# When the second layer's modulation steps run inside the first channel MLP: pace 1.0 and 0.6 in place of 0.65 and 0.72, and a rule that holds some of them back

## The chip, the cores and the metric

The kernel runs on one core of one Trainium2 chip. The time is what one execution takes on the device, in microseconds. Three executions of the kernel before took 2763.98, 2764.24 and 2766.1 us; their median is 2764.24 us.

## The reference

The reference is one step of a two-layer network over 1152 tokens (128 context tokens, 1024 latent tokens) of width 1024, all in float32. Each layer has a token mixer and then a channel MLP with a hidden width of 4096. Every sub-layer is normed, modulated, and added back through a gate:

```python
def adaln(cvec, w, b):
    m = jax.nn.silu(cvec) @ w + b
    return [t[:, None, :] for t in jnp.split(m, N_MOD, axis=-1)]

def sqrelu_mlp(h, w1, w2):
    return jnp.square(jax.nn.relu(h @ w1)) @ w2

    for i in range(DEPTH):
        sh1c, sc1c, gt1c, sh2c, sc2c, gt2c = adaln(ctx_cond, ada_w[i], ada_b[i])
        sh1l, sc1l, gt1l, sh2l, sc2l, gt2l = adaln(c, ada_w[i], ada_b[i])
        ...
        ctx = ctx + gt1c * o_ctx
        lat = lat + gt1l * o_lat
        h_ctx = rmsnorm(ctx, norm_mlp_g[i]) * (1.0 + sc2c) + sh2c
        h_lat = rmsnorm(lat, norm_mlp_g[i]) * (1.0 + sc2l) + sh2l
        ctx = ctx + gt2c * sqrelu_mlp(h_ctx, mlp_w1[i], mlp_w2[i])
        lat = lat + gt2l * sqrelu_mlp(h_lat, mlp_w1[i], mlp_w2[i])
```

The modulation (`adaln`) of the second layer depends on the conditioning vectors alone. It is a product of two vectors with a 1024 x 6144 matrix, and it is needed only when the second layer begins.

## The kernel before, in words

Activations are held transposed: eight tiles of 128 features by 1152 tokens, and the tokens in three blocks of 384 (j = 0, 1, 2). A float32 product is made of three matmuls: each operand is split in a high and a low part (ACT copies the high part, DVE subtracts it from the source to get the low part), and high x high, high x low and low x high are summed in PSUM. The helper lines are L238 (high part on ACT), L241 (low part on DVE), and L344 to L346 (the three matmuls). So every weight tile costs ACT and DVE an instruction, and so does every activation tile that a matmul reads.

**The channel MLP has two halves** (`part` 0 and 1), each a loop over 8 blocks of the hidden width. The first half (`block0`) does token block 0 in the plain way: four upward groups of 24 matmuls, then eight downward groups of 12. The second half (`block1`) does token blocks 1 and 2 together, with a seven-product scheme for the upward matmuls in place of eight. Its products have names (A11, S1, A12, S2, S4, S3, A22), two sets of seven to a block. The weight operand of a product is made by DVE from sums of weight blocks: these are the items of kind `comb`. The sums stand at L292, L293 (with A11) and at L298, L299 (with A12). The downward weights are items of kind `unit`, which need no sum. A product's result in PSUM (`quad`, three PSUM tiles to a set, out of four that the downward groups share) is read by ACT (L1300, L1304) or added to an earlier one by DVE (L1310), then passes ACT twice (relu L1269, square L1270) and becomes a high part `hidh` (ACT) and a low part `hidl` (DVE), which the downward matmuls (`bps`) read. DVE also adds each downward result to the residual (L537).

**What sets the order.** The instructions of each engine stand in the order in which this code issues them, and each engine takes its own in that order. After each product, and after each downward group or half group, `tick` is called. It splits the next weight items (up to 6 ahead in the second half, 3 in the first), takes a step of `ada` when a counter `pace` says so, and takes a step of the norm that is pending. A block of the first half has 12 ticks, a block of the second half 34: numbers 1 to 13 and 16 belong to products (`kind` 0); 14 and 15 are the first half groups of the first two downward columns (`begin`, `kind` 1); 17 to 22 are the rest of those two columns, in half groups; 23 to 34 are the other downward groups. Products and downward groups are 12 matmuls long, half groups 6. Low parts are put in a list (`late`) and issued at the next `flush`, so the `hidl` of a product stands behind the steps of the ticks up to the next product's eviction.

**A step of `ada`** is one row block of the second layer's modulation matrix: two DVE instructions (L377, `junk`<-`adav`,`bc`), each a product of a 128 x 256 tile of weights with a broadcast conditioning row, summed along the row, one for each of the two conditioning vectors; each of them is followed by an instruction that reads the accumulator. Then SP is told to load the tile for the step after the next (L409): there are two buffers for these tiles, so that load must wait until this step has read its own. There are 192 such steps. Four times, at the start of each quarter of the columns, two steps load and prepare the broadcast row `bc` (L371 on ACT, L372 on DVE). One step is taken before the blocks, so 201 calls in all run the generator to its last product. What is left after the last block would be drained at once.

SP issues all loads of weights (L232, 512 KB each) and of modulation tiles (L409, 128 KB each) in the order of the code.

Of the kernel before, what the change touches and what calls it, by code (L numbers as in the profile page):

```python
# [38 lines left out]
def kernel(  # L39
# [77 lines left out]
    items = []  # L117
# [91 lines left out]
    wst = {"load": 0, "split": 0, "use": 0}  # L209
# [120 lines left out]
    def w_ahead(depth=None, most=2):  # L330
        d = depth if depth is not None else (3 if wextra else 1)
        n = 0
        while wst["split"] < wst["use"] + d and n < most and w_split():
            n += 1
# [192 lines left out]
    def step(g):  # L527
        next(g, None)
# [10 lines left out]
    def qstep(queue):  # L539
        while queue:  # L540
            try:
                next(queue[0])
                return True
            except StopIteration:
                queue.pop(0)
        return False

    def qdrain(queue):
        while qstep(queue):
            pass  # L550
# [19 lines left out]
        return queue  # L570

    HC = {}
    ADA_PACE = (0.65, 0.72)

    def norm_t(i, j, k, t):
        l, sub = divmod(i, 2)
# [102 lines left out]
    with tc.manual_schedule():  # L679
# [579 lines left out]
        def mlp(l, pend, make_norm, yp, ada, early):  # L1259
# [13 lines left out]
            quads = {}  # L1273

            def product(part, q, name, w, tick):
                st = quads.setdefault(q, {})
                b, bank = W_H[name]
# [30 lines left out]
                else:  # L1308
                    t = st[at]
                    nc.vector.tensor_tensor(out=t, in0=p, in1=t, op=ALU.add)  # L1310
                    flush()
                    squared(at[0], at[1] + 1, t, True)
                tick(0)

            def b_mm(ps, w, j, k0=0, k1=4):
                mm3(ps, lambda k: w[0][:, k, :], lambda k: w[1][:, k, :], lambda k: hid[k, j], 4, k0, k1)

            def down(units, js, tick):
                for n in units:
                    w = w_next()  # L1320
                    for j in js:
                        ps = zps("bps")
                        b_mm(ps, w, j)
                        resid(l, 5, n, j, ps)
                        flush()
                        tick(1)
                    w_done(w)
# [4 lines left out]
            def block0(tick):  # L1332
                for n in range(4):
                    w = w_next()
                    ps = zps("aps1")
                    mm_k(ps, w, hact(0))
                    w_done(w)
                    flush()
                    t = stile("qt")
                    nc.scalar.activation(t, ps, AF.Relu)  # L1340
                    squared(n, 0, t, False)
                    tick(0)
                for p in range(4):
                    w = w_next()
                    pss = [zps("bps") for _ in range(2)]
                    for k0, k1 in ((0, 3), (3, 4)) if p == 0 else ((0, 4),):
                        for n2 in range(2):
                            b_mm(pss[n2], half_w(w, n2), 0, k0, k1)
                            if k1 < 4:
                                continue  # L1350
                            resid(l, 5, 2 * p + n2, 0, pss[n2])
                            flush()
                            tick(1)
                        flush()
                    w_done(w)

            def block1(tick, tail):
                ws, pss = [], {}

                def begin(n, j):  # L1360
                    pss[n, j] = zps("bps")
                    b_mm(pss[n, j], ws[n], j, 0, 2)
                    tick(1)

                def end(n, j):
                    b_mm(pss[n, j], ws[n], j, 2, 4)
                    resid(l, 5, n, j, pss.pop((n, j)))
                    flush()
                    tick(1)

                for q, name in UP:
                    if q != "u":
                        product(1, q, name, w_next(), tick)
                    elif not tail:
                        ws.append(w_next())
                        begin(name, 2)
                if tail:
                    return
                flush()
                for n in range(2):  # L1380
                    end(n, 2)
                for n in range(2):
                    begin(n, 1)
                    end(n, 1)
                for w in ws:
                    w_done(w)
                down(range(2, 8), (2, 1), tick)

            pace = [0.0]
# [4 lines left out]
            for part in range(2):  # L1394
                for blk in range(8):
                    last = blk == 7
                    count = [0]

                    def tick(kind):
                        count[0] += 1  # L1400
                        env["defer"] = True
                        w_ahead(*((3, 1) if part == 0 else (6, 2)))
                        env["defer"] = False
                        pace[0] += 0 if (part, blk) in ((0, 7), (1, 0)) else ADA_PACE[part]
                        if pace[0] >= 1:
                            pace[0] -= 1
                            step(ada)
                        if part == 0 and last and count[0] == 4:
                            env["room"] += 16
                        if part == 0 or blk > 0:  # L1410
                            qstep(pend)

                    if part == 0:
                        block0(tick)
                    else:
                        block1(tick, last)
                    if part == 0 or not last:
                        hid.clear()
                    if part == 0 and last:
                        qdrain(pend)  # L1420
                        pend.extend(early())
# [304 lines left out]
```

## Time and profile before

| | before |
|---|---|
| median of 3 runs | 2764.24 us (2763.98 to 2766.1) |
| the profiled execution's own time | 2765.05 us |
| its span, first to last instruction | 2763.3 us |
| PE busy (matmuls) | 2707.8 us, 98% |
| DVE busy | 1838.4 us, 67% |
| ACT busy | 1204.7 us, 44% |
| DMA, mean | 89 GB/s |
| granted TensorE clock, mean | 0.994 |

The sections of the profile used here are the windows (busy time of each engine in a stretch), the waits (engine and line, what they waited for, us in total, times, longest), the chain of waits in order of time, and the timeline of one engine (start, duration, engine, line, operation, tiles; in square brackets the idle time before it and what ended it). In the first channel MLP, the first half runs from about 841 to 1112 us of the span and the second half from about 1113 to 1596 us. The second channel MLP, which has no `ada`, has its second half from about 2233 to 2717 us. A matmul of 384 columns starts some 0.175 us after the one before it when nothing is waited for; its recorded duration of 0.34 us overlaps the next one's.

### The profile page before, as it was taken

To read this page: it belongs to the slowest core of one execution; us is meant where nothing else is said; L and a number is where in the kernel's file an instruction comes from. 1 tells how busy PE (TensorE), PEld (TensorE's weight loads), DVE (VectorE), ACT (ScalarE), POOL (GpSimd) and SP (SyncE) were. 2 spreads that over 40 slices of the span, in tenths; PEclk is the share of its full clock that TensorE was granted. 3 is DMA by queue.
4 is the path that set the end of the run, shared out by engine and by line. 5 is a ranking of instruction groups with operands and counts; after the bars stand their busy time and mean duration, and the time that the engine had idled before them with its cause. 6 is when DMAs were issued, how large, how long until landed. Compare 5 with 4: busy or idle time off the path is not lost.

```text
span 2763.3 us, 48985 instructions
## 1 busy us (share of the span) xinstructions
PE 2707.8 (98%) x19863; PEld 2633.9 (95%) x19863; DVE 1838.4 (67%) x3997; ACT 1204.7 (44%) x2118; POOL 56.0 (2%) x79
## 2 busy tenths in 40 slices
PE   7999999999999999999999999999999999999998
PEld 5999999999899999999999998999999999999998
DVE  5676777777867966687888773443675566655555
ACT  5444343343535544444444463231464454444444
POOL 0000000000000000000000000000000000000000
PEclk9999999999999999999999999999999999999999
DMA  6122211221214454233333320111234432211212
GB/s 231 52 70 62 76 57 64 69 67 60 83 59 130 154 159 148 81 104 111 111 109 119 98 71 31 61 37 39 85 122 123 129 100 76 78 62 62 69 62 69
DMA packets 113698, 245.13 MB, mean 89 GB/s; under 512 B 12736, under 2 KB 68416, under 8 KB 113472
## 3 DMA queue, kind: packets, MB, share of 16 engines
q1 hardware_dynamic: 113472, 242.00, 27.4%
q8 instruction: 156, 2.56, 0.4%
q14 instruction: 70, 0.57, 0.1%
HBM read 236.19 MB, written 5.77 MB: 88 GB/s over the span
## 4 chain that ended last, share of the span: by engine, by line
PE 85%; DVE 7%; ACT 3%; DMA 3%; issue 1%; POOL 0%; SPq 0%; POOLq 0%; DVEq 0%; ACTq 0%
PE bps L345 9%; PE bps L346 9%; PE bps L344 9%; PE zps L344 5%; PE zps L345 5%; PE quad L1287 5%; PE zps L346 5%; PE quad L1289 5%; PE quad L1288 5%; PE aps L346 3%; PE aps L345 3%; PE aps L344 3%; PE lps L893 1%; PE ups L344 1%; PE ups L346 1%
## 5 line engine op out<-in xcount | busy, mean ns | idle before, releaser
L537 DVE SCALAR_TENSOR_TENSOR x<-bps,mod,x 128x384 f32<-128x384 f32 (+2 forms) x512 | 249.1, 512 | 152.1 <-PE bps L346 150.5
L241 DVE TENSOR_TENSOR wlo<-wraw,whi 128x1024 fp32r<-128x1024 f32 x206 | 251.4, 1220 | 104.1 <-ACT whi L238 103.9
L344 PE MATMUL zps<-hh,whi 128*128 128x384 f32 x912 | 317.3, 348 | 3.2 <-ACT hh L492 3.2
L1287 PE MATMUL quad<-hc,wunit 128*128 128x384 f32 x896 | 306.0, 341 | 9.2 <-ACT qt L1300 4.8
L1289 PE MATMUL quad<-hc,wunit 128*128 128x384 f32 x896 | 304.6, 340 | 3.4 <-DVE wunit L241 3.4
L345 PE MATMUL zps<-hl,whi 128*128 128x384 f32 x912 | 306.6, 336 | 0.8 <-DVE hl L500 0.8
L346 PE MATMUL zps<-hh,wlo 128*128 128x384 f32 x912 | 306.2, 336 | 1.2 <-DVE wlo L241 1.2
L345 PE MATMUL bps<-hidl,wunit 128*128 128x384 f32 x896 | 301.1, 336 | 3.7 <-DVE hidl L241 3.7
L1288 PE MATMUL quad<-hc,wunit 128*128 128x384 f32 x896 | 303.5, 339 | 0.0
L344 PE MATMUL bps<-hidh,wunit 128*128 128x384 f32 x896 | 300.7, 336 | 0.0
L346 PE MATMUL bps<-hidh,wunit 128*128 128x384 f32 x896 | 300.6, 335 | 0.0
L238 ACT ACTIVATE wunit<-wraw 128x512 fp32r<-128x512 f32 x304 | 187.4, 624 | 246.5 <-PE bps L346 235.7
L238 ACT ACTIVATE whi<-wraw 128x1024 fp32r<-128x1024 f32 x206 | 216.9, 1053 | 131.4 <-DMA wraw<-w 84.5
L241 DVE TENSOR_TENSOR wunit<-wraw,wunit 128x512 fp32r<-128x512 f32 x304 | 205.9, 686 | 26.3 <-ACT wunit L238 26.3
L241 DVE TENSOR_TENSOR hidl<-qt,hidh 128x384 fp32r<-128x384 f32 x192 | 106.7, 556 | 171.8 <-ACT hidh L238 171.7
L345 PE MATMUL bps<-hidl,whi 128*128 128x384 f32 x640 | 215.4, 337 | 0.8 <-DVE hidl L241 0.6
L344 PE MATMUL bps<-hidh,whi 128*128 128x384 f32 x640 | 215.8, 337 | 0.0
L346 PE MATMUL bps<-hidh,wlo 128*128 128x384 f32 x640 | 215.1, 336 | 0.0
L344 PEld LDWEIGHTS zps<-hh,whi 128*128 128x128 f32 x912 | 171.7, 188 | 12.7 <-issue 4.9
L1287 PEld LDWEIGHTS quad<-hc,wunit 128*128 128x128 f32 x896 | 170.0, 190 | 13.7 <-ACT qt L1300 8.1
L345 PEld LDWEIGHTS zps<-hl,whi 128*128 128x128 f32 x912 | 171.8, 188 | 2.5 <-DVE hl L500 2.5
L1289 PEld LDWEIGHTS quad<-hc,wunit 128*128 128x128 f32 x896 | 170.0, 190 | 4.0 <-DVE wunit L241 4.0
(226 smaller groups left out, 5918.2 us busy)
## 6 DMA issues: line engine op xcount, KB each, us to landing
wraw<-w SPq DMA_DIRECT2D x256, 512.0 KB, 3.5
adav<-ada_w SPq DMA_DIRECT2D x320, 128.0 KB, 2.5
wraw<-w_in SPq DMA_DIRECT2D x40, 512.0 KB, 4.2
adar<-ada_w SPq DMA_DIRECT2D x16, 512.0 KB, 8.4
x<-xT SPq DMA_DIRECT2D x24, 192.0 KB, 4.8
x<-xT SPq DMA_DIRECT2D x8, 576.0 KB, 3.8
yT<-y SPq DMA_DIRECT2D x24, 192.0 KB, 1.9
wraw<-w_out SPq DMA_DIRECT2D x8, 512.0 KB, 3.9
```

What stands on the lines that cost most here:

```text
L238: nc.scalar.activation(w[0], src, AF.Copy)
L241: eng.tensor_tensor(out=w[1], in0=src, in1=w[0].bitcast(F32), op=ALU.subtract)
L344: nc.tensor.matmul(ps, wh(k), ah, start=(k == 0), stop=False)
L345: nc.tensor.matmul(ps, wh(k), al, start=False, stop=False)
L346: nc.tensor.matmul(ps, wl(k), ah, start=False, stop=(k == n - 1))
L537: nc.vector.scalar_tensor_tensor(out=xs, in0=ps[:, a:b], scalar=g, in1=xs, op0=ALU.mult, op1=ALU.add)
L893: nc.tensor.matmul(ps[m * b:m * b + m, i, :], lhs[:, t0:t0 + m], rhs(c, b), start=True, stop=True)
L1287: nc.tensor.matmul(p, w[0][:, k, :], bh, start=(first and k == 0), stop=False, **go)
L1288: nc.tensor.matmul(p, w[0][:, k, :], bl, start=False, stop=False, **go)
L1289: nc.tensor.matmul(p, w[1][:, k, :], bh, start=False, stop=(k == 3), **go)
```

## The change

Two numbers and one condition. In the first channel MLP the counter now grows by 1.0 instead of 0.65 with each tick of the first half, and by 0.6 instead of 0.72 with each tick of the second half (not in the last block of the first half nor in the first block of the second, as before). And in the second half a tick after a product takes no step when the weight item that was split last is a `comb`; the counter keeps what it has, so the steps are taken at later ticks, one to a tick.

```diff
-    ADA_PACE = (0.65, 0.72)
+    ADA_PACE = (1.0, 0.6)
...
                         pace[0] += 0 if (part, blk) in ((0, 7), (1, 0)) else ADA_PACE[part]
-                        if pace[0] >= 1:
+
+                        if pace[0] >= 1 and (part == 0 or kind or items[min(wst["split"], len(items)) - 1][0] != "comb"):
                             pace[0] -= 1
                             step(ada)
```

No instruction is added or taken away; `junk` steps, their loads, and the eight preparations of `bc` change their places. The places that matter are on DVE.

The head of block 3 of the second half, first the kernel before, from the last step of the block ahead of it to the first `hidl` (`wunit` is a low part of a weight operand, `wraw` and `s` are sums of weight blocks, `qt` a product's result):

```order
L377 SCALAR_TENSOR_TENSOR junk,part<-adav,bc 128x256 x2
L292 TENSOR_TENSOR s_14562<-wraw 128x512
L293 TENSOR_TENSOR wraw<-wraw 128x512
L377 SCALAR_TENSOR_TENSOR junk,part<-adav,bc 128x256 x2
L241 TENSOR_TENSOR wunit<-wraw,wunit 128x512 x3
L298 TENSOR_TENSOR wraw<-wraw 128x512
L299 TENSOR_TENSOR wraw<-wraw 128x512
L377 SCALAR_TENSOR_TENSOR junk,part<-adav,bc 128x256 x2
L1310 TENSOR_TENSOR qt<-quad,qt 128x384
L241 TENSOR_TENSOR hidl<-qt,hidh 128x384
```

and the changed kernel:

```order
L241 TENSOR_TENSOR wunit<-wraw,wunit 128x512
L292 TENSOR_TENSOR s_14688<-wraw 128x512
L293 TENSOR_TENSOR wraw<-wraw 128x512
L241 TENSOR_TENSOR wunit<-wraw,wunit 128x512 x3
L298 TENSOR_TENSOR wraw<-wraw 128x512
L299 TENSOR_TENSOR wraw<-wraw 128x512
L1310 TENSOR_TENSOR qt<-quad,qt 128x384
L241 TENSOR_TENSOR hidl<-qt,hidh 128x384
```

The steps among the sums are gone; L1310 stands directly behind L299.

The same block from its last added product (S3 of the second set, L1310) to the first residual add. The kernel before:

```order
L1310 TENSOR_TENSOR qt<-quad,qt 128x384
L241 TENSOR_TENSOR hidl<-qt,hidh 128x384
L241 TENSOR_TENSOR wunit<-wraw,wunit 128x512
L377 SCALAR_TENSOR_TENSOR junk,part<-adav,bc 128x256 x4
L241 TENSOR_TENSOR hidl<-qt,hidh 128x384
L241 TENSOR_TENSOR wunit<-wraw,wunit 128x512
L377 SCALAR_TENSOR_TENSOR junk,part<-adav,bc 128x256 x2
L241 TENSOR_TENSOR hidl<-qt,hidh 128x384
L241 TENSOR_TENSOR wunit<-wraw,wunit 128x512
L537 SCALAR_TENSOR_TENSOR x_8132<-bps,mod,x_8132 128x384
```

and the changed kernel:

```order
L1310 TENSOR_TENSOR qt<-quad,qt 128x384
L241 TENSOR_TENSOR hidl<-qt,hidh 128x384
L241 TENSOR_TENSOR wunit<-wraw,wunit 128x512
L377 SCALAR_TENSOR_TENSOR junk,part<-adav,bc 128x256 x6
L241 TENSOR_TENSOR hidl<-qt,hidh 128x384
L241 TENSOR_TENSOR wunit<-wraw,wunit 128x512
L377 SCALAR_TENSOR_TENSOR junk,part<-adav,bc 128x256 x2
L241 TENSOR_TENSOR hidl<-qt,hidh 128x384
L241 TENSOR_TENSOR wunit<-wraw,wunit 128x512
L537 SCALAR_TENSOR_TENSOR x_8132<-bps,mod,x_8132 128x384
```

Three steps now stand ahead of the second `hidl` (that of S3) where there were two.

In the first half, a stretch of downward groups in block 2 (`hc` and `nt` belong to the pending norm). The kernel before:

```order
L537 SCALAR_TENSOR_TENSOR x_8132<-bps,mod,x_8132 128x256
L241 TENSOR_TENSOR hc<-nt,hc 128x384
L609 TENSOR_TENSOR ht<-nt,ht 128x384
L537 SCALAR_TENSOR_TENSOR x_8133<-bps,mod,x_8133 128x128
L537 SCALAR_TENSOR_TENSOR x_8133<-bps,mod,x_8133 128x256
L241 TENSOR_TENSOR wlo<-wraw,whi 128x1024
L377 SCALAR_TENSOR_TENSOR junk,mod<-adav,bc 128x256 x2
```

and the changed kernel:

```order
L537 SCALAR_TENSOR_TENSOR x_8132<-bps,mod,x_8132 128x256
L377 SCALAR_TENSOR_TENSOR junk,mod<-adav,bc 128x256 x2
L241 TENSOR_TENSOR hc<-nt,hc 128x384
L609 TENSOR_TENSOR ht<-nt,ht 128x384
L537 SCALAR_TENSOR_TENSOR x_8133<-bps,mod,x_8133 128x128
L537 SCALAR_TENSOR_TENSOR x_8133<-bps,mod,x_8133 128x256
L241 TENSOR_TENSOR wlo<-wraw,whi 128x1024
L377 SCALAR_TENSOR_TENSOR junk,mod<-adav,bc 128x256 x2
```

Every group's residual add now has a step behind it.

## The prediction

> **What bounds the kernel now.** I read the windows first, one for each half of the first channel MLP without its ends, and one for the second half of the other MLP, which has no modulation steps (columns: PE, PEld, DVE, ACT, POOL busy, granted clock, DMA share, GB/s).
>
> ```profile
> 874.00:1076.00 202.00, 202.00 (x1156) 202.00 (x1156) 156.88 (x392) 102.06 (x155) 0.00 (x0) 1.00 0.50 156
> 1145.00:1575.00 430.00, 421.73 (x2412) 417.96 (x2411) 343.77 (x981) 182.03 (x349) 0.00 (x0) 1.00 0.35 110
> 2260.00:2700.00 440.00, 438.39 (x2519) 436.32 (x2518) 258.25 (x433) 191.09 (x369) 0.00 (x0) 1.00 0.22 70
> ```
>
> PE sets the time in all three. Only the second has an idle PE that the steps could have caused: 8.3 us in 430, against 1.6 in 440 where there are none. The first half has no idle PE at all. So the most that moving steps can gain is about 8 us, 0.3% of the kernel. The waits of PE in that second window are two (us in total, times, longest):
>
> ```profile
> PE quad L1287 <- ACT qt L1300: 4.6, 5, 1.8
> PE bps L345 <- DVE hidl L241: 3.7, 5, 1.2
> ```
>
> Call them the head wait (a product waits for PSUM to be read) and the hid wait (a downward group waits for `hidl`). A modelled end makes each 0.17 us shorter than what it costs, so the ten of them cost 5.4 and 4.5 us. The chain of waits shows the head wait of block 3 (start, us, what):
>
> ```profile
> 1316.64 0.87 DVE junk L377 x4
> 1317.50 1.75 DVE wunit L241 x3
> 1319.25 0.61 DVE wraw L298
> 1319.89 0.69 DVE wraw L299
> 1320.58 0.79 DVE junk L377 x4
> 1321.37 0.42 DVE qt L1310
> ...
> 1323.93 0.39 ACT qt L1300
> 1324.37 0.44 PE quad L1287
> ```
>
> DVE is late with L1310 by its sums and by two steps (0.87 and 0.79 us with their accumulator reads); ACT, in order, reaches L1300 only behind what L1310 feeds. The hid wait of the same block, on DVE:
>
> ```profile
> 1341.49 0.56 DVE L1310 TENSOR_TENSOR qt<-quad,qt 128x384 f32<-128x384 f32 x1
> ...
> 1342.43 0.68 DVE L241 TENSOR_TENSOR wunit<-wraw,wunit 128x512 fp32r<-128x512 f32 x1
> 1343.44 0.43 DVE L377 SCALAR_TENSOR_TENSOR junk<-adav,bc 128x256 f32<-128x256 f32 x1 [0.32 <-DMA adav<-ada_w]
> ...
> 1345.37 0.43 DVE L377 SCALAR_TENSOR_TENSOR junk<-adav,bc 128x256 f32<-128x256 f32 x1 [1.06 <-DMA adav<-ada_w]
> ...
> 1346.10 0.55 DVE L241 TENSOR_TENSOR hidl<-qt,hidh 128x384 fp32r<-128x384 f32 x1
> ...
> 1347.76 0.43 DVE L377 SCALAR_TENSOR_TENSOR junk<-adav,bc 128x256 f32<-128x256 f32 x1 [0.51 <-DMA adav<-ada_w]
> ...
> 1348.50 0.55 DVE L241 TENSOR_TENSOR hidl<-qt,hidh 128x384 fp32r<-128x384 f32 x1
> ```
>
> Here it is not the steps' own 0.8 us that hold `hidl` up, but their loads: DVE stands in order behind a tile that is not there. With two buffers the load for a step can go out only when the step two before it is done.
>
> **The change part by part.** It moves 30 steps. In the first half 84 ticks count, so 54 steps become 84; 201 are needed in all, one comes ahead, so 146 in the second half become 116. No instruction goes away.
>
> *Head of the blocks, a gain.* Ticks 1 to 7 of blocks 1 to 6 take no step now, so both steps of that chain go. Block 3 has the longest wait (1.8 and 0.17 us), and without 0.87 + 0.79 it would lose 0.35; the other four share 3.4 us, and 0.8 or more less would leave them little. I take 0.4 left of 5.4: **-5.0 us**. It cannot gain more than 5.4.
>
> *Behind product S3, a loss.* The pause leaves 3 to 5 steps in the counter; they come out one to a tick, in ticks 8, 9 and 11 to about 20. That puts steps 13, 14 and 15 ahead of S3's `hidl` (the x6 row of the order), where one or two stood. The third needs a load that goes out when the first is done. In block 3 the trace shows when such a third step runs: the first (begun at 1343.44) was done 0.8 us later at 1344.3, its buffer's next step began at 1347.76 after a wait for the load, and DVE was free again at 1348.50. With the change `hidl` takes that place. PE's rows of the wait before:
>
> ```profile
> 1346.02 0.34 PE L344 MATMUL bps<-hidh,wunit 128*128 128x384 f32 x1
> 1346.71 0.44 PE L345 MATMUL bps<-hidl,wunit 128*128 128x384 f32 x1 [0.35 <-DVE hidl L241]
> ...
> 1539.57 0.34 PE L344 MATMUL bps<-hidh,wunit 128*128 128x384 f32 x1
> 1540.55 0.45 PE L345 MATMUL bps<-hidl,wunit 128*128 128x384 f32 x1 [0.64 <-DVE hidl L241]
> ```
>
> PE wanted it at 1346.20 (1346.02 and 0.175) and got it 0.61 us after `hidl` began (1346.10 to 1346.71). So it would get it at 1348.50 + 0.61 = 1349.11 and lose 2.9 us where it lost 0.5. In block 6 the first step's buffer was asked for anew and filled at
>
> ```profile
> 1537.48 5.38 SPq L409 DMA_DIRECT2D adav<-ada_w  x3
> 1541.62 0.43 DVE L377 SCALAR_TENSOR_TENSOR junk<-adav,bc 128x256 f32<-128x256 f32 x1 [0.52 <-DMA adav<-ada_w]
> ```
>
> that is 4.1 us on, behind a weight load of 512 KB that goes out just before it; with 0.74 for the step and 0.61 PE starts at 1542.97 in place of 1539.75 and loses 3.2. Block 4 has the preparation of a new `bc` row in ticks 14 and 15 in place of two steps, and waits for the row's load instead, which I count alike. Six blocks at 3.05 us are 18.3, less the 4.5 of before: **+13.8 us**. The bounds are those of the load:
>
> ```profile
> DMA to landing us min/median/max: 1.9/2.5/5.8
> ```
>
> With 2.5 in place of 3.5 to 4.1 a block loses about 1.5 (9 in all, +4.5); with 5.8 about 4.8 (29, +24). I take the rows of that very place.
>
> *The clock.* A PE that idles 2.7 us at a stretch six times is new in this MLP. Rows of elsewhere show what follows such a gap (PE's starts with the idle time ahead of them, and windows, where the granted clock stands third from the end):
>
> ```profile
> 47.68 1.13 PE L470 MATMUL rp<-rq,sel_sb 128*128 128x96 f32 x8 [2.13 <-DVE rq L463]
> ...
> 48.00:50.00 2.00, 2.00 (x16) 2.00 (x15) 0.62 (x2) 0.51 (x2) 0.00 (x0) 1.00 0.00 0
> ...
> 56.45 0.69 PE L344 MATMUL zps<-hh,whi 128*128 128x384 f32 x1 [2.06 <-ACT hh L492]
> ...
> 56.00:58.00 2.00, 1.51 (x4) 1.11 (x5) 1.84 (x4) 1.39 (x3) 0.47 (x2) 0.58 0.00 0
> 58.00:60.00 2.00, 2.00 (x8) 2.00 (x7) 2.00 (x4) 1.23 (x2) 0.81 (x1) 0.57 0.00 0
> ...
> 1116.57 0.41 PE L1287 MATMUL quad<-hc,wunit 128*128 128x384 f32 x1 [1.65 <-DVE x L537]
> ...
> 1118.84 0.69 PE L1289 MATMUL quad<-hc,wunit 128*128 128x384 f32 x1 [1.68 <-DVE wunit L241]
> ...
> 1122.20 0.52 PE L1287 MATMUL quad<-hc,wunit 128*128 128x384 f32 x1
> 1122.53 0.52 PE L1288 MATMUL quad<-hc,wunit 128*128 128x384 f32 x1
> ...
> 1124.00:1126.00 2.00, 2.00 (x12) 2.00 (x11) 1.44 (x3) 0.39 (x1) 0.00 (x0) 0.83 0.60 156
> ```
>
> A gap of 2.13 us left the clock at 1.00. One of 2.06 halved it: 0.58 and 0.57 as the means of two windows of 2 us are 3.4 us at 0.50. Two gaps close together, 3.3 us idle in all, halved it till about 1124.7 (0.83 is 0.7 us at 0.50), some 6 us from PE's start at 1118.84. At half clock matmuls start 0.32 us apart (1122.20 to 1122.53) in place of 0.175, so 3.4 us at half clock cost 1.5 and 6 us cost 2.7. Gaps of 2.7 lie between; I take three in four to halve it, 1.75 us each: 4.5 x 1.75 = **+7.9 us** (bounds 0 and 6 x 2.7 = 16). [...]
>
> *The first half.* 30 steps more at 0.85 us are 25 us of DVE in its seven counted blocks, 3.6 us in each block of 33.6. PE hides them where DVE has room. Block 2 is the tightest:
>
> ```profile
> 907.20:940.80 33.60, 33.60 (x194) 33.60 (x193) 31.38 (x79) 18.80 (x31) 0.00 (x0) 1.00 0.51 157
> ```
>
> 31.4 + 3.6 = 35.0 is 1.4 over, and what is over makes a `hidl` or a residual add late. Four PSUM tiles of 2.1 us each give some slack, and later blocks have room. I take **+1.5 us** (0 to 5).
>
> *Behind the hid wait.* Steps of ticks 16 to 21 come every 1.05 us, and the loads give one in about 2.4 (two buffers, 4 + 0.85 us a round). So residual adds (L537) fall some 6 us behind, which three more PSUM tiles just cover: **+0.8 us** (0 to 6). SP stands at these loads too, in order, with weight loads behind it:
>
> ```profile
> SPq L409 <- DVE junk L377: 244.7, 135, 22.0
> ```
>
> It did so before, and no engine waits for a weight load in this half (they are split six items ahead), so I put nothing on it.
>
> Sum, from the profiled execution's own 2765.05 us: -5.0 + 13.8 + 7.9 + 1.5 + 0.8 = +19.0, so 2784. The median of the runs shown lies 0.8 under that execution, which gives **2783 us**, 0.7% slower.
>
> **The rivals.** *The stalls come, the clock stays.* For it: the gap of 2.13 us did not lower it. Against: the one of 2.06 did. Without the 7.9 the time is 2775. [...] *The load is quick, nothing changes:* at 2.5 us a block loses 1.5, a gap too short for the clock: -5.0 + 4.5 + 1.5 = +1, 2765. For it: 2.5 is the median of all these loads. Against: rows of this very place show 3.5 to 4.1, and the weight load ahead of them stays. *Faster:* the pause lets DVE run ahead, and both buffers are full when the burst begins. If the third step needed no wait, three steps of 0.8 us would end 1.55 + 2.5 us after L1310 began, and `hidl` 0.55 later, at 4.6; PE wants it 4.7 after (1341.49 to 1346.20). Then both waits go: -5.0 - 4.5 + 1.5 = -8, 2756. Against: two buffers hold two tiles, and S3's L1310 cannot come sooner than S3. It decides if the load takes under 1 us. *Worse:* the first half overflows by 5, the residual adds by 6, and every gap halves the clock for 6 us: 2783 + 3.5 + 5.2 + 8.3 = 2800. *The change does not do what it says* (steps are left over and drained at the end): excluded, since the order has the last step in block 6.
>
> **How the numbers follow.** The forecast 0.50, clock stays 0.17, no change 0.13, faster 0.08, worse 0.12. A difference of 0.2% (5.5 us) is about what a measurement of this kernel can tell from none. Slower by more than that: 0.50 + 0.17 + 0.12, and a little of the quick load, 0.80; within it 0.12; faster 0.08. The range 2769 to 2798 holds the forecast with its bounds, the clock that stays and half of the worse case.
>
> **What would show it.** Right: the head wait (`quad` for ACT L1300) nearly gone in blocks 1 to 6; the hid wait (`bps` L345 for `hidl`) at 6 times, near 2.7 us each; three steps in a row ahead of it, the third waiting for `adav`; the clock under 1.00 in windows behind most of them; the idle PE of 874 to 1076 still under 2 us. Wrong: a hid wait of 1 us or none would fell the main term, a clock of 1.00 throughout the second one, and new waits in the first half or on PSUM behind L537 would mean that those terms are too small.

## The result, and the profile after

| | before | after |
|---|---|---|
| median, runs on the same chip | 2764.85 us (6 runs) | 2784.33 us (6 runs, 2783.6 to 2786.99) |
| ratio | | 1.0073, 95% interval 1.0063 to 1.0083 |
| profiled execution's own time | 2765.05 us | 2784.22 us |
| its span | 2763.3 us | 2782.4 us |
| PE busy | 2707.8 us | 2717.9 us |
| granted TensorE clock, mean | 0.994 | 0.99 |

The changed kernel is 0.7% slower: 2784.33 us where 2783 was predicted.

The three windows of the kernel after stand first: the first half of the first channel MLP, its second half, and the second half of the other MLP (columns: PE, PEld, DVE, ACT, POOL busy with the number of instructions, granted clock, DMA share, GB/s).

```profile
874.00:1076.00 202.00, 200.57 (x1143) 199.10 (x1143) 171.75 (x484) 100.99 (x155) 0.00 (x0) 1.00 0.55 171
1145.00:1590.00 445.00, 427.24 (x2400) 423.69 (x2399) 324.22 (x858) 182.80 (x351) 0.00 (x0) 0.98 0.31 98
2280.00:2720.00 440.00, 438.39 (x2519) 436.31 (x2518) 258.14 (x434) 191.14 (x368) 0.00 (x0) 1.00 0.21 70
```

The first half carries the added steps (DVE 171.75 us where it was 156.88 in as long a window) with 1.4 us of idle PE. The second half has 17.8 us of idle PE in 445 us, against 8.3 in 430 before, at a lower clock. The third window, which the change doesn't touch, is as it was. So the time went into the second half, and there in two ways. The waits of PE in it are these (us in total, times, longest):

```profile
PE bps L345 <- DVE hidl L241: 17.5, 6, 3.4
PE quad L1287 <- ACT qt L1300: 0.3, 1, 0.3
```

The head wait is gone but for 0.3 us. The hid wait has grown from 3.7 to 17.5 us, once in each of blocks 1 to 6. Block 3 shows how, first on DVE (start, duration, engine, line, operation, tiles; in brackets the idle time ahead and what ended it):

```profile
1349.11 0.56 DVE L1310 TENSOR_TENSOR qt<-quad,qt 128x384 f32<-128x384 f32 x1
...
1351.28 0.43 DVE L377 SCALAR_TENSOR_TENSOR junk<-adav,bc 128x256 f32<-128x256 f32 x1 [0.54 <-DMA adav<-ada_w]
...
1353.11 0.43 DVE L377 SCALAR_TENSOR_TENSOR junk<-adav,bc 128x256 f32<-128x256 f32 x1 [0.96 <-DMA adav<-ada_w]
...
1356.05 0.43 DVE L377 SCALAR_TENSOR_TENSOR junk<-adav,bc 128x256 f32<-128x256 f32 x1 [2.07 <-DMA adav<-ada_w]
...
1356.79 0.56 DVE L241 TENSOR_TENSOR hidl<-qt,hidh 128x384 fp32r<-128x384 f32 x1
```

Three steps stand ahead of `hidl`, each behind a load of its own; the third waits longest, 2.07 us. PE, at the same place:

```profile
1353.64 0.34 PE L344 MATMUL bps<-hidh,wunit 128*128 128x384 f32 x1
1357.40 0.44 PE L345 MATMUL bps<-hidl,wunit 128*128 128x384 f32 x1 [3.42 <-DVE hidl L241]
```

It wanted `hidl` at 1353.64 + 0.175 and began at 1357.40, so it lost 3.58 us. The chain of waits (start, us, what) runs through the load:

```profile
1353.11 0.89 DVE junk L377 x4
1354.01 2.28 DMA adav<-ada_w
...
1356.93 0.42 DVE hidl L241
1357.40 0.44 PE bps L345
```

The second way is the clock. These windows lie behind the gap of block 3 (1357.40) and that of block 5 (1493.40):

```profile
1356.00:1360.00 4.00, 2.60 (x11) 2.60 (x12) 3.95 (x13) 0.00 (x0) 0.00 (x0) 0.83 0.18 40
1360.00:1364.00 4.00, 4.00 (x19) 4.00 (x19) 2.37 (x11) 0.63 (x1) 0.00 (x0) 0.74 0.69 221
1492.00:1496.00 4.00, 2.60 (x15) 2.60 (x16) 3.94 (x13) 0.00 (x0) 0.00 (x0) 1.00 0.21 56
1496.00:1500.00 4.00, 4.00 (x25) 4.00 (x24) 2.31 (x10) 1.27 (x2) 0.00 (x0) 1.00 0.70 212
```

Behind block 3's gap the granted clock is 0.83 and 0.74 as means of 4 us, that is 3.4 us at half clock. Behind block 5's gap, of 3.00 us idle, it stays at 1.00. Behind the other four gaps it was halved too, for 3.4 us each: the mean is 0.79 in 1219 to 1227 and 1424 to 1432 us, and 0.83 in 1288 to 1298 and 1556 to 1566 us.

### The profile page after: what moved, and what is told of

It reads as the page before. It is cut to its first block, busy times and chain, and to the rows that moved or that the text cites. A ratio compares the mean times of both kernels' runs of the same rounds, so it can differ in the third digit from the quotient of the medians.

```text
span 2782.4 us, 49004 instructions
## 1 busy us (share of the span) xinstructions
PE 2717.9 (98%) x19863; PEld 2642.1 (95%) x19863; DVE 1841.2 (66%) x3997; ACT 1204.6 (43%) x2118; POOL 55.7 (2%) x79
## 4 chain that ended last, share of the span: by engine, by line
PE 83%; DVE 8%; ACT 3%; DMA 3%; issue 2%; SPq 0%; POOL 0%; POOLq 0%; DVEq 0%; ACTq 0%
PE bps L345 9%; PE bps L346 9%; PE bps L344 8%; PE zps L344 5%; PE quad L1287 5%; PE quad L1289 5%; PE quad L1288 5%; PE zps L345 5%; PE zps L346 5%; PE aps L346 3%; PE aps L345 3%; PE aps L344 3%; PE lps L893 1%; PE ups L344 1%; PE ups L346 1%
## 5 line engine op out<-in xcount | busy, mean ns | idle before, releaser
L537 DVE SCALAR_TENSOR_TENSOR x<-bps,mod,x 128x384 f32<-128x384 f32 (+2 forms) x512 | 250.1, 513 | 160.1 <-PE bps L346 158.8
L345 PE MATMUL bps<-hidl,wunit 128*128 128x384 f32 x896 | 304.6, 340 | 17.5 <-DVE hidl L241 17.5
L346 PE MATMUL bps<-hidh,wunit 128*128 128x384 f32 x896 | 304.0, 339 | 0.0
L344 PE MATMUL bps<-hidh,wunit 128*128 128x384 f32 x896 | 303.9, 339 | 0.0
L345 PEld LDWEIGHTS bps<-hidl,wunit 128*128 128x128 f32 x896 | 170.6, 190 | 19.4 <-DVE hidl L241 19.4
L377 DVE SCALAR_TENSOR_TENSOR junk<-adav,bc 128x256 f32<-128x256 f32 x384 | 155.6, 448 | 36.2 <-DMA adav<-ada_w 35.9
L1287 PEld LDWEIGHTS quad<-hc,wunit 128*128 128x128 f32 x896 | 169.3, 189 | 9.6 <-ACT qt L1300 3.8
```

Of the source, the lines that this page charges most:

```text
L344: nc.tensor.matmul(ps, wh(k), ah, start=(k == 0), stop=False)
L345: nc.tensor.matmul(ps, wh(k), al, start=False, stop=False)
L346: nc.tensor.matmul(ps, wl(k), ah, start=False, stop=(k == n - 1))
L377: nc.vector.scalar_tensor_tensor(out=junk_tile(), in0=raw, scalar=1.0, in1=bc[:, c * 256:(c + 1) * 256], op0=ALU.mult, op1=ALU.mult, accum ...
L537: nc.vector.scalar_tensor_tensor(out=xs, in0=ps[:, a:b], scalar=g, in1=xs, op0=ALU.mult, op1=ALU.add)
L1287: nc.tensor.matmul(p, w[0][:, k, :], bh, start=(first and k == 0), stop=False, **go)
```

## The experiments

Theory: the hold rule lets the counter fill up and pay out in a burst, so a third step stands ahead of S3's `hidl`; DVE waits in order for that step's load; PE waits for `hidl`; and the idle PE lowers the clock for a while. Rivals: the new pace overloads the first half; the load is not to blame but the steps' own work; the clock is a side show.

**Each part alone.** First the pace without the rule, as an edit of the changed kernel:

```diff
-                        if pace[0] >= 1 and (part == 0 or kind or items[min(wst["split"], len(items)) - 1][0] != "comb"):
+                        if pace[0] >= 1:
```

> The kernel before with the two numbers 1.0 and 0.6 alone, without the rule that holds steps back. Theory (the rule makes the bursts, the bursts make the hid wait and the low clock): in the second half the steps stay spread, 20.4 in a block of 34 ticks, mostly one or two of ticks 13 to 15, so the hid wait stays at or under the 4.5 us of before, the head wait falls from 5.4 to 3 or 4, no clock falls in blocks 1 to 6; with about 1.5 us more in the first half the time is 2763 us, within 2 of the kernel before. Rival (30 more steps in the first half cost the time): about 2780, with new waits between 840 and 1112 us.

Measured: 2762.05 us, ratio 0.9993 to the kernel before (0.9984 to 1.0002). The waits of PE in its second half:

```profile
PE quad L1287 <- ACT qt L1300: 2.7, 4, 1.0
PE bps L345 <- DVE hidl L241: 1.0, 1, 1.0
```

Both are smaller than before, with 30 steps fewer in this half, and the clock of the window is 1.00. Of the five head waits of before, only the longest, that of block 3, is gone; the other four lose what they lost. The first half loses 2.6 us with the 30 steps more, where it lost 0.8. So the pace by itself costs nothing, and the rival that the first half is overloaded falls.

Then the rule with the old pace:

```diff
-    ADA_PACE = (1.0, 0.6)
+    ADA_PACE = (0.65, 0.72)
```

> The rule alone, with the old numbers 0.65 and 0.72. Theory: the first half stays as before (0.8 us lost); in the second half the head wait is near 0.4 us and the same three steps stand ahead of S3's low part, so the hid wait is 17 to 19 us and five or six of its gaps halve the clock (about 7 us); more steps in ticks 16 to 28 put the residual adds further behind, 0 to 8 us on PSUM. Time 2784 to 2792 us. Rival (the first half makes the loss): 2764 or less.

Measured: 2782.37 us, ratio 1.0068 (1.0053 to 1.0083). The waits of PE in its second half:

```profile
PE bps L345 <- DVE hidl L241: 14.0, 6, 2.8
PE quad L1287 <- ACT qt L1300: 2.5, 3, 1.9
PE bps L344 <- DVE x L537: 0.2, 1, 0.2
```

The rule alone brings the six hid waits and five stretches at half clock, four of them behind hid waits (gaps of 2.76, 2.32, 2.09 and 2.06 us) and one behind the longest head wait (1.94 us); PE's starts are 0.32 us apart in them. Two things missed. The time lies 2 us under what was expected, and the hid waits lose 14.9 us instead of 17 to 19. And a head wait stays in three places, the longest of 1.9 us, in block 3. No step stands among the sums there either; at the end of block 2, DVE waited 5.13 us for a new `bc` row:

```profile
1319.17 0.42 DVE L372 TENSOR_TENSOR bc<-bc,row 128x256 f32<-128x256 f32 x1 [5.13 <-ACT bc L371]
```

Three residual adds, a step and the sums of block 3 then followed without a pause, so L1310 began only at 1327.86. With the new pace no row falls there, and the wait is gone. The other two head waits are of 0.3 us, like the one in the changed kernel. The rule is the cause of the loss.

**The third step.** The rule plus no step in ticks 14 and 15, so the burst stops ahead of S3's `hidl`:

```diff
-                        if pace[0] >= 1 and (part == 0 or kind or items[min(wst["split"], len(items)) - 1][0] != "comb"):
+                        if pace[0] >= 1 and (part == 0 or count[0] not in (14, 15)) and (part == 0 or kind or items[min(wst["split"], len(items)) - 1][0] != "comb"):
```

> The changed kernel, with no step in ticks 14 and 15 either: only the step of tick 13 stands ahead of S3's low part. Theory: the hid wait goes (18.4 us less), and with it the low clock (7.5 us less), so 2758 us; but the steps of ticks 16 to 22 now come in a burst, seven in 7.4 us of PE where the loads allow one in 2.4 us, and if the residual adds fall more than three PSUM tiles (6.3 us) behind, PE waits for PSUM 1 to 3 us a block: up to 2775 us. Rival (the loss is not at that place): 2784.

Measured: 2757.51 us, ratio 0.9975 (0.9966 to 0.9984). The window and the waits of its second half:

```profile
1145.00:1590.00 445.00, 444.28 (x2548) 441.99 (x2548) 336.72 (x884) 198.44 (x381) 0.00 (x0) 1.00 0.32 101
...
PE quad L1287 <- DVE qt L1310: 0.6, 1, 0.6
PE quad L1287 <- ACT qt L1300: 0.5, 2, 0.3
PE bps L345 <- DVE hidl L241: 0.2, 1, 0.2
```

The same steps are all taken, a few ticks later. PE is idle for 0.7 us of 445 instead of 17.8 (the wait of 0.6 us lies behind the window, at 1594), the clock is 1.00, and the kernel is 26.8 us faster than with the change, or 25.8 when each is taken against the kernel before on its own chip. The hid waits (18.4 us) and the clock (7.5 us) make 25.9. No wait for PSUM appears behind L537, although two steps more are now put off to the ticks behind.

**The load against the work.** The changed kernel with only the first two modulation tiles loaded, and the steps' DVE work left in:

```diff
+        have = []
...
-            raw = pool.tile([128, 256], F32, tag="ada", name="adav", bufs=2)
-            nc.sync.dma_start(out=raw, in_=ada_w1[qt, s][:, 0])
-            return raw
+            if len(have) < 2:
+                raw = pool.tile([128, 256], F32, tag="ada", name="adav", bufs=2)
+                nc.sync.dma_start(out=raw, in_=ada_w1[qt, s][:, 0])
+                have.append(raw)
+                return raw
+            return have[s % 2]
```

> The changed kernel, where all but the first two loads of modulation tiles are left out: each step reads one of two tiles that are there, so the second layer's modulation is computed from the wrong weights. All steps stand where they stood. Theory (the loads hold the third step up, not the steps' own time): three steps of 0.8 us end just before S3's low part is wanted, the hid wait falls to 2 us or less in all, the clock stays at 1.00: 2757 us. Rival (the steps' own time on DVE): the hid wait stays near 1.6 us a block, 2766 us or more.

Measured: 2761.62 us, ratio 0.9988 (0.9979 to 0.9997). The hid wait in its second half, then the longer of the two on PE, and DVE ahead of it:

```profile
PE bps L345 <- DVE hidl L241: 3.1, 2, 2.5
...
1411.21 0.69 PE L345 MATMUL bps<-hidl,wunit 128*128 128x384 f32 x1 [2.53 <-DVE hidl L241]
...
1409.93 0.76 DVE L372 TENSOR_TENSOR bc<-bc,row 128x256 f32<-128x256 f32 x2 [3.42 <-ACT bc L371]
1410.61 0.55 DVE L241 TENSOR_TENSOR hidl<-qt,hidh 128x384 fp32r<-128x384 f32 x1
```

With the same DVE order and no loads, four of the six hid waits are gone and a fifth is 0.7 us. The work of the steps is thus not the cause; their loads are. The expectation missed by 4.6 us, and 4.2 of it is block 4: there the preparation of the `bc` row stands in ticks 14 and 15, its own load was left in, and DVE waited 3.42 us for it. That wait cost 2.7 us and a stretch at half clock 1.5 us (PE's starts 0.32 us apart from 1411.70 us on).

**Three tiles in place of two.** All loads stay, but a step's tile is asked for three steps ahead. (The identity matrix is moved to another pool to make room.)

```diff
...
-            raw = pool.tile([128, 256], F32, tag="ada", name="adav", bufs=2)
+            raw = pool.tile([128, 256], F32, tag="ada", name="adav", bufs=3)
...
-        return ada_vec(1, 0, load, bc_tile, part, junk_tile, 2)
+        return ada_vec(1, 0, load, bc_tile, part, junk_tile, 3)
...
```

> The changed kernel with three buffers for the modulation tiles in place of two, and loads three steps ahead (the room comes from the identity matrix, which is moved to a pool that is freed after the first layer's mixer). Theory: the load for the third step of the burst goes out when the step of tick 12 is done, 2 us sooner, so the hid wait falls from 2.9 to about 0.6 us a block, too short for the clock: 2784 - 14 - 7.5 = 2762 us. Rival (SP or DMA, not the number of buffers, sets the wait): 2780 or more.

Measured: 2764.12 us, ratio 0.9995 (0.9985 to 1.0005). The waits in its second half, where these lines stand one lower than elsewhere, and block 4 on DVE and PE:

```profile
PE bps L344 <- DVE hidl L240: 5.1, 4, 3.5
...
1411.10 0.42 DVE L371 TENSOR_TENSOR bc<-bc,row 128x256 f32<-128x256 f32 x1 [4.12 <-ACT bc L370]
...
1412.70 0.44 PE L344 MATMUL bps<-hidl,wunit 128*128 128x384 f32 x1 [3.54 <-DVE hidl L240]
```

One more buffer takes the change from +19.5 us to nothing: three blocks lose 0.7 us each, two lose nothing, and only block 4 with its row, which the expectation left out, keeps the long wait (3.70 us lost) and the half clock behind it (PE's starts 0.32 us apart from 1413.74 to 1416.94 us). With two buffers the load of a third step can't go out before the first step is done; that is the wait, and it has now been taken away by the buffer alone.

**Both mends together**, three tiles and no step in ticks 14 and 15:

> The changed kernel with three buffers and no step in ticks 14 and 15. Theory: no hid wait, no head wait, no low clock, and the loads give a step in 1.6 us, so that the residual adds stay within PSUM: 2757 us, 0.3% faster than the kernel before. If the burst behind tick 15 still ends on PSUM: 2760 to 2765.

Measured: 2756.55 us, ratio 0.9970 (0.9958 to 0.9981), the fastest kernel of this study. Its second half up to the end of block 6, and what is left of its waits (its lines, too, stand one off):

```profile
1145.00:1565.00 420.00, 419.74 (x2410) 417.96 (x2409) 322.83 (x860) 182.67 (x350) 0.00 (x0) 1.00 0.33 104
...
PE quad L1288 <- DVE qt L1311: 0.7, 1, 0.7
PE quad L1288 <- ACT qt L1301: 0.3, 1, 0.3
```

That is 0.3 us of idle PE in 420. The third tile adds little to the two held ticks (2757.51 without it, on another chip).

**The clock by itself.** To part the stall from the clock, PE was to be kept busy through the wait: the changed kernel with matmuls whose results nobody reads, ahead of the one that waits. The first try had 14 of them, in a PSUM tile of the pool (tag `g`) that the steps' `junk` tiles use:

```diff
+                if l == 0 and len(pss) == 2 and blk_now[0] > 0:
+                    d = gps("fill")
+                    src = hid[0, 2][0]
+                    for _ in range(14):
+                        nc.tensor.matmul(d, ws[0][0][:, 0, :], src, start=True, stop=True)
                 for n in range(2):
                     end(n, 2)
...
```

> The changed kernel, with 14 matmuls more in each block 1 to 6 that compute nothing needed, just ahead of the half group that waits for S3's low part (2.45 us, 84 matmuls in all). Theory (the gap alone halves the clock): the wait of PE there shrinks to about 0.6 us, the added matmuls run in time that was idle, the clock stays at 1.00, and the time falls by about 7 us to 2777. Rival (the clock falls for another reason, or is not worth that much): 2784 or more.

Measured: 2798.79 us, ratio 1.0128 (1.0111 to 1.0145). The wait in its second half:

```profile
PE fill L1384 <- DVE junk L377: 16.3, 5, 3.8
```

The test was flawed. The added matmuls had to wait for a tile that the steps held, so the gap only moved ahead of them, and their 84 x 0.175 = 14.7 us came on top. It can't part the stall from the clock, though its gaps serve in the last section. The second try puts them in the PSUM tile that the next half group overwrites anyway:

```diff
-                    pss[n, j] = zps("bps")
+                    if (n, j) not in pss:
+                        pss[n, j] = zps("bps")
...
+                if l == 0 and blk_now[0] > 0:
+                    d = pss[0, 1] = zps("bps")
+                    for _ in range(14):
+                        nc.tensor.matmul(d, ws[0][0][:, 0, :], hid[0, 2][0], start=True, stop=True)
                 for n in range(2):
                     end(n, 2)
...
```

> As the run fill, but the 14 added matmuls of a block write the PSUM tile that the next half group overwrites, so they wait for no step of the modulation. Theory: they fill 2.45 us of each gap of 2.2 to 3.4, the wait of PE for S3's low part falls to about 0.2 to 1 us a block, the clock stays at 1.00 in blocks 1 to 6, and the time falls by 7 us to 2777, though 84 matmuls are added. Rival (the clock term is not real, or the half clock has another cause): no fall, 2784 or more.

Measured: 2780.62 us, ratio 1.0051 (1.0035 to 1.0068). The window and the wait of its second half:

```profile
1145.00:1590.00 445.00, 438.83 (x2511) 435.33 (x2511) 326.19 (x863) 184.12 (x353) 0.00 (x0) 1.00 0.32 99
...
PE bps L345 <- DVE hidl L241: 5.9, 6, 1.3
```

Six gaps remain, of at most 1.35 us, and the clock is 1.00 throughout. The added matmuls (14.7 us) and what is left of the wait (6.85 us lost) make 21.6 us, 3.1 more than the wait of 18.4 that they replace; nevertheless the kernel is 3.7 us faster than with the change. With the clock's 7.5 us taken off, 3.1 - 7.5 = -4.4 was to be expected. (Against the kernel before, timed on the same chips, it stands 5.7 us better than the change.) So the clock's share is real, and of the size that was put on it. The expectation of 2777 took the gaps that are left as smaller.

The same with 6 matmuls a block leaves a gap in between:

```diff
-                    for _ in range(14):
+                    for _ in range(6):
```

> The same with 6 added matmuls in a block (1.05 us), so that gaps of 1.2 to 2.4 us are left. [...] If only a gap's own length counts and about 2 us is enough, four or five do: 2783.

Measured: 2783.32 us, ratio 1.0062 (1.0047 to 1.0077). The gaps of blocks 3 and 6, and the windows behind them:

```profile
1359.17 0.45 PE L345 MATMUL bps<-hidl,wunit 128*128 128x384 f32 x1 [1.82 <-DVE hidl L241]
...
1562.86 0.44 PE L345 MATMUL bps<-hidl,wunit 128*128 128x384 f32 x1 [1.16 <-DVE hidl L241]
...
1360.00:1364.00 4.00, 4.00 (x16) 4.00 (x15) 4.00 (x16) 0.00 (x0) 0.00 (x0) 0.58 0.53 156
...
1562.00:1566.00 4.00, 3.14 (x18) 3.14 (x19) 4.00 (x15) 0.12 (x1) 0.00 (x0) 1.00 0.23 70
```

On record for this run stood also 2777 to 2780 us, with none to two blocks at half clock, and that was a miss: the gaps were 2.64, 1.94, 1.82, 2.95, 1.80 and 1.16 us, and all but the last halved the clock. Here gaps of 1.82 and 1.80 us were enough (a mean of 0.58 in 1360 to 1364 and 0.57 in 1496 to 1500 us). The time is that of the expectation's 2783 us, for which four or five blocks were to halve the clock by the length of their gaps; the last section shows why length alone can't be the rule.

## Why the prediction was right, term by term

| term | predicted | measured in the profile after |
|---|---|---|
| head wait | -5.0 | -4.9 (0.42 us left) |
| hid wait | +13.8 | +13.9 (18.4 lost, 4.5 before) |
| the clock | +7.9 | +7.5 |
| the first half | +1.5 | +1.1 in its waits (1.9 lost, 0.8 before) |
| behind the hid wait | +0.8 | 0 |
| sum | +19.0 | +17.6 |

- **Head wait: the number right, the reason for block 3 not.** ACT reaches L1300 in time in all blocks but one. In blocks 1, 2, 4 and 6 it is the rule that does it: these four lost 3.4 us before and in the run with the pace alone, and 0.9 with the rule alone. Block 3's 2.0 us were put down to the two steps among its sums. But ahead of them, in the kernel before, stands a row:

```profile
1311.08 0.43 DVE L372 TENSOR_TENSOR bc<-bc,row 128x256 f32<-128x256 f32 x1 [4.58 <-ACT bc L371]
```

From there DVE has no pause up to L1310. The pace alone takes the row away from this place and the wait with it, though one of the two steps still stands among the sums; the rule alone takes the steps away and leaves 2.1 us. So these 2.0 us came of the pace, by a row that the prediction counted only where it arrived, in block 4.
- **Hid wait: right, with its mechanism.** Blocks 1 to 6 lost 3.12, 2.84, 3.58, 3.40, 3.16 and 2.34 us; the two estimates of 2.9 and 3.2 lie among them. (The row of 1.9, 2.5 and 5.8 us that gave this term its bounds holds the first layer's loads too; the 192 loads of L409 alone took 1.9, 2.2 and 4.9 us. The estimate itself didn't rest on it.) That it is the load of the third step was argued from the trace before; the runs without loads and with a third tile show it. Counting block 4's row preparation as a load of the same length was right too (3.40), and these two runs, in which it was nearly all that remained, show it apart.
- **The clock: the size right, the count a little low.** Three gaps in four were to halve it, at 1.75 us each; it was five in six, at 1.68, 1.45, 1.45, 1.45 and 1.45 us (ten starts 0.32 us apart in place of 0.175 make 1.45). The rival in which the clock stays (2775) is refuted by the half clock behind five of the six gaps, and by the 3.7 us that added matmuls won back. Shorter gaps than those the term was put on halved the clock too: 1.80, 1.82 and 1.94 us with 6 added matmuls, 1.94, 2.06 and 2.09 us with the rule alone, and 2.19 us in the kernel after. The bound of 0 and the share of three in four were the author's estimates; no run shows a share that would hold elsewhere.
- **The first half: right.** Three hid waits of 0.6 to 0.7 us in it, and no other; from its first matmul to the first product of the second half (841.49 to 1112.66 us before, 843.52 to 1116.44 after) it takes 1.75 us more, so some 0.6 us lies in delays that the waits don't list. The pace alone makes the kernel no slower.
- **Behind the hid wait: too large.** No residual add made PE wait for PSUM. The tiles cover the delay, as the working said they just might.
- **What no term held.** The terms make +17.6 and the spans differ by 19.1 us. The first MLP began 2.0 us later (843.5 in place of 841.5), with the code ahead of it unchanged, and a stretch at half clock in block 0, there before as well, cost 1.1 us less (from PE's starts at 1118.84 before and 1122.66 after, the next 30 starts took 8.01 and 6.90 us). Together that is 18.5, so 0.6 us net has no name. Part of the closeness of the total is therefore luck: the late beginning made up for terms that were put too high.

The other rivals fall too. *The load is quick:* each of the six blocks lost 2.3 to 3.6 us, not 1.5. *Faster:* the third step waited in each of the five blocks that have one there, and in block 4 the row did. It was the right idea at the wrong place, since with the burst cut short of S3's `hidl` the kernel reached 2757.5, next to that rival's 2756. *Worse:* neither the first half nor the residual adds overflowed, and no stretch at half clock in these blocks of the kernel after came near 6 us (3.4 each).

## What to carry to other kernels

Work that is held back comes out in a burst: count how many items of the burst stand, in their engine's order, ahead of the next result on the critical path, and compare with the number of buffers that feed them. With two buffers the third item must wait until a load that goes out behind the first has landed, however little the engine has to do: here 2.07 us in block 3, for a step of 0.89 us. And look at the granted clock behind each stall of PE: here 18.4 us of stalls, in six gaps of 2.19 to 3.42 us, brought another 7.5 us at half clock behind five of them.

## What the runs showed of the hardware

A gap's own length doesn't decide whether the clock drops. Three rows of PE in the run with the rule alone, and two of the run with 6 added matmuls:

```profile
1331.00 0.44 PE L1287 MATMUL quad<-hc,wunit 128*128 128x384 f32 x1 [1.94 <-ACT qt L1300]
1356.98 0.44 PE L345 MATMUL bps<-hidl,wunit 128*128 128x384 f32 x1 [2.43 <-DVE hidl L241]
1490.30 0.45 PE L345 MATMUL bps<-hidl,wunit 128*128 128x384 f32 x1 [2.33 <-DVE hidl L241]
```

```profile
1428.03 0.53 PE L345 MATMUL bps<-hidl,wunit 128*128 128x384 f32 x1 [2.95 <-DVE hidl L241]
1495.78 0.45 PE L345 MATMUL bps<-hidl,wunit 128*128 128x384 f32 x1 [1.80 <-DVE hidl L241]
```

The gaps of 1.94, 2.95 and 1.80 us halved the clock: PE's starts were 0.32 us apart from 1331.89 to 1335.09 us behind the first, and the mean clock was 0.57 in 1428 to 1432 and in 1496 to 1500 us behind the others. Those of 2.43 and 2.33 us, and the one of 3.00 us in block 5 of the change, didn't: the starts stayed 0.175 us apart behind the first two, and the clock was 1.00 in 1492 to 1500 us behind the third.

Nor did the clock come back at a set time after the gap. PE's starts went back from 0.32 to 0.175 us apart at 1225.39, 1293.73, 1362.02, 1430.30 and 1563.29 us in the kernel after, which is 4.53, 4.59, 4.62, 4.79 and 4.39 us from the ends of the five gaps; here is one of these moments:

```profile
1361.38 0.52 PE L345 MATMUL bps<-hidl,wunit 128*128 128x384 f32 x1
1361.70 0.50 PE L346 MATMUL bps<-hidh,wunit 128*128 128x384 f32 x1
1362.02 0.35 PE L344 MATMUL bps<-hidh,wunit 128*128 128x384 f32 x1
1362.22 0.34 PE L345 MATMUL bps<-hidl,wunit 128*128 128x384 f32 x1
```

In the run with 6 added matmuls the same took 3.48, 4.01, 3.54 and 4.08 us in blocks 2 to 5. What was alike in the five stretches of the kernel after is their length, 3.4 us, and the clock in them: 0.50 in 1223 to 1225, 1291 to 1293, 1359 to 1361, 1428 to 1430 and 1561 to 1563 us.

Two rows of the first run with 14 added matmuls add to this:

```profile
1219.24 2.73 PE L1384 MATMUL fill<-hidh,wunit 128*128 128x384 f32 x14 [2.76 <-DVE junk L377]
1289.18 4.24 PE L1384 MATMUL fill<-hidh,wunit 128*128 128x384 f32 x14 [3.46 <-DVE junk L377]
```

The first 14 matmuls ran at full clock (2.73 us; 1.00 in 1220 to 1224 us), the second at half in part (4.24 us; 0.74 in 1288 to 1292 us). The gap of 3.83 us in block 3 of that run halved the clock too (0.70 in 1360 to 1364 us). So in these executions a gap of 1.80 us halved the clock and gaps of 2.76 and 3.00 us left it. What decides, apart from a gap's length, they don't show, and no run was made to test it. Five of six halved is thus the count of one execution, and another may have a different one.
